# Sample tokens in four groups, their rows of u and v spread over all four stretches of a mixer

## Chip, core and metric

One core of a Trainium2 chip runs the whole program in one launch. The metric is the device time of that launch in microseconds (us).

## What is computed

One inference step of a two-layer encoder for 384 tokens: 256 of one prompt and 128 sample tokens (8 streams of 16). Layer 0 has a state-space block, layer 1 an attention block, and behind each stands the mixer that this change is about, with 16384 experts, each a row of a table `u` and a row of a table `v` of 1024 numbers:

```python
q = (xb @ w_q).reshape(PEER_TOKEN_BLOCK, PEER_HEADS, PEER_QDIM)
...
vs, ci = lax.top_k(cand, PEER_TOPK)
...
eid = (e1 * PEER_NKEYS + e2).reshape(PEER_TOKEN_BLOCK, PEER_HEADS * PEER_TOPK)
gate = jax.nn.softmax(vs.astype(jnp.float32), axis=-1).reshape(PEER_TOKEN_BLOCK, PEER_HEADS * PEER_TOPK)
ue = jnp.take(u_tab, eid, axis=0)
act = jax.nn.gelu(jnp.einsum('tkd,td->tk', ue, xb).astype(jnp.float32))
ve = jnp.take(v_tab, eid, axis=0)
return jnp.einsum('tk,tkd->td', (gate * act).astype(xb.dtype), ve)
```

Each token picks 128 experts, takes the product of each one's row of `u` with the token, and sums the rows of `v` with the weights that come out.

## The kernel before, in words

**The prompt's 256 tokens** go through all 16384 experts. The experts are a grid of 128 by 128; `e2` counts 128 slices of 128 experts, and `HE` is 64. A *u step* (`u_step`) multiplies one slice of `u` with the tokens and writes one of 64 rows of an expert grid, `G[0]` for the first 64 steps and `G[1]` for the other 64, each row 128 experts by 256 tokens. A *v step* (`v_step`) reads one row of the grid and adds its product with a slice of `v` to four accumulators in PSUM. So a mixer has 256 steps `s` in **four stretches** of 64: stretch 1 fills `G[0]`, stretch 2 `G[1]`, stretch 3 uses up `G[0]`, stretch 4 `G[1]`. Between the steps of stretch 2, every second step, `w_step` multiplies columns of `G[0]` with the gates of the experts that each token chose (0 elsewhere); in stretch 3 it does so for `G[1]`.

Numbers are kept at full precision by splitting: a slice of 512 KB is loaded to `raw` (three buffers, SP queue), ScalarE (ACT) rounds it to `hi` (L105), VectorE (DVE) makes the rest `lo` (L106), and TensorE (PE) multiplies three times: 24 products of 256 columns in a u step (L130 to L132), 12 of 512 columns in a v step (L143). Steps listed in `NATIVE` (8 of a mixer's first 64) multiply the raw slice without a split: 8 products (L1098), each of which the trace shows as 2.

**The 128 sample tokens** gather the rows that they chose. A *u item* is one gather of 128 rows (512 KB, issued by GpSimd, POOL, L1035) to one of three buffers `gath`, and one instruction of DVE that multiplies them with the tokens and sums (L1072). There are 128 of them in a mixer, in `GR` groups of tokens: a group's u items must all be done before `group_end` makes the coefficients of that group. A *quad* (`v_quad`) takes four gathers of rows of `v` and adds 8 products with small coefficient tiles to the banks `out_s` (L1089); there are 32 quads. Their buffers are `gv` (4) and later `gath`.

**Order.** Each engine runs its instructions in the order of its queue. Which step issues how many u items and quads is set in the code: `tick` issues `RATES` u items a step as soon as the routing of the sample tokens has ended (some 16 steps into stretch 1) until all 128 are done; `quads` issues one quad every 3.75 steps from the third step of stretch 3 to the end. The routing of the prompt's tokens (top 16 of scores and their decoding, all on DVE) is pulled in pieces between the steps of stretch 1. A scheduler with a model of the engines fixes the final order of what the code leaves open.

Of the kernel before, what the change touches and what calls it, by code (L numbers as in the profile page):

```python
# [9 lines left out]
F32 = mybir.dt.float32  # L10
# [9 lines left out]
P = 128  # L20
# [21 lines left out]
GR = 2  # L42
TG = P // GR
RG = 32 // GR
TURN = 6
GSCALE = 2.0 ** 15
NATIVE = range(4, 58, 7)
# [6 lines left out]
RATES = (0.95, 0.8, 0.8)  # L54
QUADS = (2, 3.75)
# [3 lines left out]
def encoder_step(ctx: ExitStack, tc: tile.TileContext, t_in, t_out):  # L59
# [750 lines left out]
    def peer(l):  # L810
        with ExitStack() as c:
# [32 lines left out]
            xg = [T(x0ctx.__enter__(), [P, D], F32, tag="xg0"), T(one, [P, D], F32, tag="xg1")]  # L844
# [13 lines left out]
            for g in range(GR):  # L858
                rows = xrow[g]
                pool.dma_start(xg[g], bass.AP(tensor=rows.tensor, offset=rows.offset, ap=[[0, GR], [D, TG], [1, D]]))  # L860

# [170 lines left out]
            pools = {}  # L1032
# [11 lines left out]
            def fetch_v(n):  # L1044

                if n < P:
                    r, q = divmod(n, 4)
                    if done["u"] == P and n % 7 >= 4:
                        tile_ = T(one, [P, D], F32, tag="gath", bufs=3)
                    else:  # L1050
                        tile_ = T(pools["gv"], [P, D], F32, tag="gv", bufs=4)
                    vrows[n] = gather(tile_, t_in["p_v"], eidT[:, 32 * q + r:32 * q + r + 1])
# [3 lines left out]
            def group_end(g, lay):  # L1056
# [5 lines left out]
                a = coef[g] = T(one, [P, TG], F32, tag="a", bufs=2)  # L1062
# [4 lines left out]
            def u_item(k):  # L1067
# [6 lines left out]
                if j == TG - 1:  # L1074
                    lay = T(one, [P, GR, TG], F32, tag="cm", bufs=2)
# [4 lines left out]
            def v_quad(r):  # L1080
# [5 lines left out]
                rows = [vrows.pop(4 * r + q) for q in range(4)]  # L1086
# [64 lines left out]
            due_u = [0.0]  # L1151

            def tick(rate):
                due_u[0] += rate
                while done["u"] < min(int(due_u[0]), P):
# [20 lines left out]
            for e2 in range(HE):  # L1176
# [170 lines left out]
```

## Time and profile before

| | us |
|---|---|
| Median of 3 runs (2600.17 to 2608.42) | 2606.8 |
| The profiled execution, whole | 2607.89 |
| Its span, first to last instruction | 2605.9 |
| Stretches 1, 2, 3, 4 of the first mixer | 224.4, 214.2, 251.5, 214.9 |
| The same of the second mixer | 228.6, 214.5, 256.2, 215.1 |

The profiled execution lies 1.1 us above the median; 2.0 us of it lie outside its span. The stretches are cut where the first steps of each begin on the engines, to within 3 us. What lies before, between and behind the mixers is the same code in both kernels.

### The profile page before, as it was taken

What the parts mean: (1) busy time and instruction counts of PE and PEld (TensorE: products, weight loads), DVE (VectorE), ACT (ScalarE), POOL (GpSimd) and SP (SyncE); (2) the same over time, 40 slices, a digit from 0 to 9 for tenths busy, and PEclk for the clock granted to TensorE, in tenths of its full rate; (3) what the DMA queues carried; (4) which work ended last, traced back from release to release, by engine and by line L of the source; (5) the groups of instructions that cost most, each with busy time, mean ns of one, the idle gap of its engine ahead of it and who ended that gap; (6) DMA issues with size and microseconds to landing.
All of it is one profiled execution on the core that took longest, in us unless ns stands there. A gap on an engine that the chain in (4) does not pass through costs nothing. (4 is left out here: it accounts for less than half of the span.)

```text
span 2605.9 us, 45142 instructions
## 1 busy us (share of the span) xinstructions
PE 2454.3 (94%) x16792; PEld 2076.6 (80%) x16792; DVE 1942.3 (75%) x4301; ACT 1324.6 (51%) x2562; POOL 671.6 (26%) x722
## 2 busy tenths in 40 slices
PE   7999999989899989999999899999889998899998
PEld 7999988988899966666667678998789986566666
DVE  6877737989899988765555555989989998665555
ACT  5665524433466655554444453434456766464444
POOL 2222200033322244333220000023332234432331
PEclk9999999999999999999999789999999999999999
DMA  5544434478788899888886204477788898988886
GB/s 181 175 150 174 147 133 146 157 274 282 262 302 292 293 338 344 333 306 301 328 299 182 77 30 148 135 260 279 258 281 282 295 337 314 340 295 301 320 322 235
DMA packets 180428, 645.62 MB, mean 248 GB/s; under 512 B 24496, under 2 KB 27664, under 8 KB 177552
## 3 DMA queue, kind: packets, MB, share of 16 engines
q1 hardware_dynamic: 102320, 372.16, 41.0%
q0 software_dynamic: 77888, 270.58, 29.8%
q8 instruction: 131, 2.15, 0.3%
q14 instruction: 89, 0.73, 0.1%
HBM read 626.43 MB, written 18.06 MB: 247 GB/s over the span
## 5 line engine op out<-in xcount | busy, mean ns | idle before, releaser
L105 ACT CAST hi<-raw 128x1024 fp32r<-128x1024 f32 (+1 forms) x616 | 641.4, 1042 | 657.7 <-PE bank L131 403.4
L106 DVE TENSOR_TENSOR lo<-raw,hi 128x1024 fp32r<-128x1024 f32 (+1 forms) x616 | 748.8, 1216 | 237.2 <-ACT hi L105 224.6
L1035 POOL DMA_INDIRECT gath<-in_p_u,eidU x256 | 303.7, 1186 | 804.2 <-DVE gath L1072 437.4
L132 PE MATMUL bank<-xhi,lo 128*128 128x256 f32 (+1 forms) x1344 | 408.6, 305 | 9.8 <-DVE lo L106 9.6
L130 PE MATMUL bank<-xhi,hi 128*128 128x256 f32 (+1 forms) x1344 | 404.4, 301 | 11.0 <-ACT hi L105 11.0
L131 PE MATMUL bank<-xlo,hi 128*128 128x256 f32 (+1 forms) x1344 | 398.9, 297 | 0.0
L132 PE MATMUL bank<-qhi,lo 128*128 128x256 f32 (+1 forms) x1152 | 350.2, 306 | 24.9 <-DVE lo L106 24.7
L130 PE MATMUL bank<-qhi,hi 128*128 128x256 f32 (+1 forms) x1152 | 349.7, 304 | 24.3 <-ACT hi L105 17.4
L1072 DVE SCALAR_TENSOR_TENSOR gath<-gath,xg 128x1024 f32<-128x1024 f32 x256 | 311.3, 1216 | 48.2 <-DMA gath<-in_p_u,eidU 48.1
L131 PE MATMUL bank<-qlo,hi 128*128 128x256 f32 (+1 forms) x1152 | 346.1, 300 | 0.0
L143 PE MATMUL bank<-lo,phi 128*128 128x512 f32 x1024 | 331.6, 405 | 10.6 <-DVE lo L106 7.7
L143 PE MATMUL bank<-hi,plo 128*128 128x512 f32 x1024 | 322.5, 397 | 0.0
L143 PE MATMUL bank<-hi,phi 128*128 128x512 f32 x1024 | 292.5, 406 | 16.0 <-ACT hi L105 12.2
L105 ACT CAST phi<-G 128x256 fp32r<-128x256 f32 x256 | 103.4, 405 | 376.1 <-PE bank L143 259.2
L1035 POOL DMA_INDIRECT gv<-in_p_v,eidT x180 | 196.1, 1089 | 321.9 <-PE bank L1089 271.5
L132 PEld LDWEIGHTS bank<-xhi,lo 128*128 128x128 f32 x1344 | 255.4, 190 | 18.2 <-DVE lo L106 15.0
L130 PEld LDWEIGHTS bank<-xhi,hi 128*128 128x128 f32 x1344 | 256.0, 190 | 16.3 <-ACT hi L105 13.1
L143 PEld LDWEIGHTS bank<-hi,phi 128*128 128x128 f32 x1024 | 186.7, 189 | 94.6 <-ACT hi L105 40.0
L131 PEld LDWEIGHTS bank<-xlo,hi 128*128 128x128 f32 x1344 | 255.9, 190 | 0.2
L132 PEld LDWEIGHTS bank<-qhi,lo 128*128 128x128 f32 x1152 | 224.8, 196 | 31.5 <-DVE lo L106 31.1
L130 PEld LDWEIGHTS bank<-qhi,hi 128*128 128x128 f32 x1152 | 225.4, 196 | 28.0 <-ACT hi L105 20.2
L143 PEld LDWEIGHTS bank<-lo,phi 128*128 128x128 f32 x1024 | 186.7, 189 | 70.0 <-DVE lo L106 17.4
(327 smaller groups left out, 3937.7 us busy)
## 6 DMA issues: line engine op xcount, KB each, us to landing
raw<-in_u_t SPq DMA_DIRECT2D x256, 512.0 KB
raw<-in_p_v SPq DMA_DIRECT2D x256, 512.0 KB
raw<-in_w_in SPq DMA_DIRECT2D x32, 512.0 KB
raw<-in_p_w_q SPq DMA_DIRECT2D x32, 512.0 KB
s<-in_state_ssm SPq DMA_DIRECT2D x8, 1024.0 KB
raw<-in_w_z SPq DMA_DIRECT2D x16, 512.0 KB
out_sm_ssm<-s SPq DMA_DIRECT2D x8, 1024.0 KB
raw<-in_w_out SPq DMA_DIRECT2D x16, 512.0 KB
```

Source lines behind the costliest of these rows:

```text
L105: act.copy(hi, raw)
L106: dve.tensor_tensor(lo, raw, hi32, op=OP.subtract)
L130: pe.matmul(ps, whi[:, s], xhi[:, k, c0:c1], start=(k == 0), stop=False)
L131: pe.matmul(ps, whi[:, s], xlo[:, k, c0:c1], start=False, stop=False)
L132: pe.matmul(ps, wlo[:, s], xhi[:, k, c0:c1], start=False, stop=(k == KD - 1))
L143: mm = pe.matmul(ps, x, w[:, hf * n:(hf + 1) * n], start=s_, stop=e_)
L1035: pool.indirect_dma_start(out=tile_, out_offset=None, in_=tab, in_offset=bass.IndirectOffsetOnAxis(ap=idx, axis=0))
L1072: pin(dve.scalar_tensor_tensor(tile_, tile_, 1.0, xg[g], op0=OP.mult, op1=OP.mult, accum_out=au[g][:, j:j + 1]))
```

## The change

Tokens of the samples stand in four groups of 32 in place of two of 64 (`GR`), and each group's token rows are loaded when the group two before it has ended (`load_group`), into the buffer that this one held. When a u item or a quad is issued is now a table by step: `U_DUE` asks for 26 u items by the end of stretch 1, 70 by the end of stretch 2, 106 by the end of stretch 3, and the rest by step 214; `V_DUE` places 5 quads at steps 82 to 106 (stretch 2), 8 at 148 to 186 (stretch 3) and 19 at 193 to 248 (stretch 4). Rows of `v` land in rows of the expert grid that hold nothing at that time: in stretch 2 in the last 16 rows of `G[1]`, which u steps fill from step 112 on, and from step 145 on in rows of `G[0]` that v steps have used up, 4 buffers first and 8 from step 164 on. The pool `gv` is gone, and so is the use of `gath` for `v`. `NATIVE` has 18 steps (every third) in place of 8. The banks `out_s` are taken at the start of stretch 2. The copies of the tokens that stretch 2 uses are spread over 8 steps, and the residual `h` comes back over POOL's queue in place of SP's.

```diff
-GR = 2
+GR = 4
-TURN = 6
+TURN = 8
-NATIVE = range(4, 58, 7)
+NATIVE = range(3, 56, 3)
-RATES = (0.95, 0.8, 0.8)
-QUADS = (2, 3.75)
+U_DUE = ((64, 26), (128, 70), (192, 106), (214, P))
+V_DUE = [82 + 6 * i for i in range(5)] + [148 + int(5.5 * i) for i in range(8)] + [193 + int(3.1 * i) for i in range(19)]
+V_FIRST = 5
...
-            xg = [T(x0ctx.__enter__(), [P, D], F32, tag="xg0"), T(one, [P, D], F32, tag="xg1")]
+            x0pool = x0ctx.__enter__()
...
+            def load_group(g):
+                xg[g] = T((x0pool, one)[g % 2], [P, D], F32, tag=f"xg{g % 2}", bufs=1)
                 rows = xrow[g]
                 pool.dma_start(xg[g], bass.AP(tensor=rows.tensor, offset=rows.offset, ap=[[0, GR], [D, TG], [1, D]]))
...
-            def fetch_v(n):
...
+            def fetch_v(n, s):
+
+                half, e = (1, HE - 16 + 4 * (n % 4)) if s < 2 * HE else (0, 4 * (n % v_bufs(s)))
+                assert all(k != (half, e) for k, _ in vrows.values())
+                tile_ = G[half][:, e:e + 4].rearrange("p e t -> p (e t)")
+                r, q = divmod(n, 4)
+                vrows[n] = (half, e), gather(tile_, t_in["p_v"], eidT[:, 32 * q + r:32 * q + r + 1])
+
+            def v_bufs(s):
+                return 4 if s < 2 * HE + 36 else 8
...
                 if j == TG - 1:
+                    if g + 2 < GR:
+                        load_group(g + 2)
...
-            def quads(e2):
-
-                while done["v"] < min(32, int((e2 - QUADS[0]) / QUADS[1] + 1)):
+            def quads(s):
+
+                while done["v"] < 32 and V_DUE[done["v"]] <= s:
                     v_quad(done["v"])
                     done["v"] += 1
-                    ahead = 4 * done["v"] + (7 if done["u"] == P else 4)
-                    while done["f"] < min(ahead, P):
-                        fetch_v(done["f"])
-                        done["f"] += 1
+                if s >= 2 * HE - 16 and done["f"] == 4 * V_FIRST and s < 2 * HE + 17:
+                    return
+                last = 4 * V_FIRST if s < 2 * HE else P
+                ahead = 4 * done["v"] + (4 if s < 2 * HE else v_bufs(s))
+                while done["f"] < min(ahead, last):
+                    fetch_v(done["f"], s)
+                    done["f"] += 1
...
-                    sync.dma_start(h, spill)
+                    pool.dma_start(h, spill)
```

Two places in the order of the engines. The first is DVE's queue in the middle of stretch 1 of the first mixer, where pieces of the prompt's routing stand between the splits of the slices (`lo<-raw,hi`) and the u items (`gath,au<-gath,xg`). Before:

```order
L874 MAX_INDEX CI_6252<-VS_6251,tk_1026_6310 128x8
L1072 SCALAR_TENSOR_TENSOR gath_6193,au_5499<-gath_6193,xg_635_4059 128x1024
L106 TENSOR_TENSOR lo_6505<-raw_6502,hi_6504 128x1024
L872 MATCH_REPLACE tk_1050_6451<-v_1049_6450,bank_6447 128x128
L870 MAX v_1049_6450<-bank_6447 128x8
L874 MAX_INDEX IX_6253<-v_1033_6354,tk_1040_6396 128x8
L1072 SCALAR_TENSOR_TENSOR gath_6316,au_5499<-gath_6316,xg_635_4059 128x1024
L894 TENSOR_TENSOR cand_6437<-v_1033_6354 128x32
L106 TENSOR_TENSOR lo_6575<-raw_6572,hi_6574 128x1024
```

Now:

```order
L1080 SCALAR_TENSOR_TENSOR gath_6183,au_5473<-gath_6183,xg_645_4125 128x1024
L902 TENSOR_TENSOR cand_6374<-v_1025_6294 128x32
L108 TENSOR_TENSOR lo_6413<-raw_6410,hi_6412 128x1024
L878 MAX VS_6141<-cand_6374 128x8
L108 TENSOR_TENSOR lo_6461<-raw_6458,hi_6460 128x1024
L879 MAX_INDEX CI_6142<-VS_6141,cand_6374 128x8
L880 MATCH_REPLACE tk_1038_6378<-VS_6141,cand_6374 128x88
L881 MAX VS_6141<-tk_1038_6378 128x8
L882 MAX_INDEX CI_6142<-VS_6141,tk_1038_6378 128x8
L878 MAX v_1042_6399<-bank_6396 128x8
L879 MAX_INDEX IX_6143<-v_1042_6399,bank_6396 128x8
```

Where two splits came with two u items, they come with one, and routing stands in the place of the other.

The second is POOL's queue in the first mixer, where each row is a gather of 512 KB (`x4`: four of them one behind the other), at the place where the gathers of `u` end. Before, that is in stretch 3:

```order
L1035 DMA gath_12113<-in_p_u,eidU_4006 128x1024
L1035 DMA gath_12138<-in_p_u,eidU_4006 128x1024
L1035 DMA gv_12083<-in_p_v,eidT_4011 128x1024
L1035 DMA gv_12085<-in_p_v,eidT_4011 128x1024
L1035 DMA gv_12087<-in_p_v,eidT_4011 128x1024
L1035 DMA gv_12089<-in_p_v,eidT_4011 128x1024
L1035 DMA gath_12379<-in_p_v,eidT_4011 128x1024
```

Now, in stretch 4, where the gathers of `u` go on to step 214:

```order
L1042 DMA G_619_4015<-in_p_v,eidT_4011 128x1024 x4
L1042 DMA gath_13307<-in_p_u,eidU_4006 128x1024
L1042 DMA gath_13346<-in_p_u,eidU_4006 128x1024
L1042 DMA gath_13371<-in_p_u,eidU_4006 128x1024
L1042 DMA G_619_4015<-in_p_v,eidT_4011 128x1024 x4
L1042 DMA gath_13396<-in_p_u,eidU_4006 128x1024
L1042 DMA gath_13435<-in_p_u,eidU_4006 128x1024
L1042 DMA gath_13460<-in_p_u,eidU_4006 128x1024
```

Before, only gathers of `v` follow from here to the end of stretch 4; now three gathers of `u` stand between each four of `v` in the first third of stretch 4, and the gathers of `v` write the grid.

## Rows read from the trace of the kernel before

**Rows 1.** Page: engine, busy time, share of the span and instructions.

```profile
PE 2454.3 (94%) x16792; PEld 2076.6 (80%) x16792; DVE 1942.3 (75%) x4301; ACT 1324.6 (51%) x2562; POOL 671.6 (26%) x722
```

**Rows 2.** Windows: mixer 1's stretches, mixer 2's first, third; length, busy, clock, DMA share, GB/s.

```profile
483.00:707.40 224.40, 204.49 (x1521) 196.49 (x1520) 202.72 (x650) 93.79 (x143) 68.35 (x49) 0.96 0.77 260
707.40:921.60 214.20, 207.59 (x2048) 202.09 (x2047) 198.95 (x306) 142.93 (x291) 56.57 (x56) 0.99 0.87 293
921.60:1173.10 251.50, 234.65 (x1517) 159.10 (x1518) 192.04 (x323) 143.27 (x282) 106.06 (x96) 0.99 0.90 331
1173.10:1388.00 214.90, 212.74 (x1026) 149.55 (x1025) 110.57 (x147) 94.25 (x133) 63.09 (x73) 1.00 0.85 302
...
1677.00:1905.60 228.60, 205.31 (x1519) 196.99 (x1519) 203.28 (x651) 93.41 (x143) 65.59 (x49) 0.96 0.75 256
...
2120.10:2376.30 256.20, 235.48 (x1517) 159.13 (x1518) 192.13 (x323) 143.09 (x281) 104.80 (x96) 0.98 0.89 325
```

**Rows 3.** Timeline of PE: start, length, instruction, at five places of mixer 1.

```profile
534.79 3.62 PE L1098 MATMUL bank<-xf,raw 128*128 128x256 f32 x16
...
538.37 0.28 PE L130 MATMUL bank<-qhi,hi 128*128 128x256 f32 x1
...
801.28 0.28 PE L130 MATMUL bank<-xhi,hi 128*128 128x256 f32 x1
...
803.65 0.28 PE L132 MATMUL bank<-xhi,lo 128*128 128x256 f32 x1
...
807.15 0.64 PE L1131 MATMUL bank<-og,oa 128*128 128x64 f16 x16
...
807.63 0.36 PE L132 MATMUL bank<-xhi,lo 128*128 128x256 f32 x1
...
1180.62 1.09 PE L143 MATMUL bank<-hi,phi 128*128 128x512 f32 x4
...
1183.42 1.09 PE L143 MATMUL bank<-hi,phi 128*128 128x512 f32 x4
...
1189.11 0.62 PE L1089 MATMUL bank<-gv,cm 128*32 128x512 f32 x2
...
1190.96 1.20 PE L143 MATMUL bank<-hi,phi 128*128 128x512 f32 x4
```

**Rows 4.** Windows, shorter: two parts of stretch 1, four of stretch 3.

```profile
483.00:532.60 49.60, 47.42 (x373) 46.00 (x372) 40.72 (x137) 23.63 (x34) 6.34 (x5) 1.00 0.64 217
532.60:707.40 174.80, 157.07 (x1151) 150.49 (x1150) 162.00 (x514) 70.16 (x110) 62.01 (x44) 0.95 0.80 272
...
920.00:940.00 20.00, 17.75 (x112) 12.62 (x111) 16.23 (x29) 11.24 (x23) 11.64 (x11) 1.00 0.99 372
...
977.20:1060.00 82.80, 76.29 (x479) 52.33 (x478) 69.64 (x117) 45.22 (x87) 42.96 (x36) 1.00 0.95 352
...
1040.00:1060.00 20.00, 19.02 (x89) 13.69 (x88) 15.12 (x23) 7.66 (x12) 12.59 (x10) 1.00 1.00 382
...
1100.00:1173.10 73.10, 73.10 (x460) 49.20 (x459) 47.92 (x77) 42.52 (x80) 21.38 (x22) 1.00 0.88 310
```

**Rows 5.** Groups by line on DVE: count, busy, mean ns; stretch 1 twice, stretch 3.

```profile
L106 DVE TENSOR_TENSOR lo<-raw,hi 128x1024 fp32r<-128x1024 f32 x56 | 68.0, 1215 | 1.9 <-ACT hi L105 1.8
L1072 DVE SCALAR_TENSOR_TENSOR gath<-gath,xg 128x1024 f32<-128x1024 f32 x46 | 55.7, 1212 | 15.6 <-DMA gath<-in_p_u,eidU 15.6
...
L1072 DVE SCALAR_TENSOR_TENSOR gath<-gath,xg 128x1024 f32<-128x1024 f32 x28 | 34.2, 1220 | 2.5 <-DMA gath<-in_p_u,eidU 2.5
```

**Rows 6.** Waits in stretch 1 of mixer 1: total us, times, longest.

```profile
ACT hi L105 <- DMA raw<-in_u_t: 24.4, 12, 3.7
...
PEld bank L132 <- DVE lo L106: 16.0, 15, 3.1
```

**Rows 7.** Windows of L1035, POOL's gathers: stretches 3 and 4, busy and count.

```profile
921.60:1173.10 251.50, 106.06 (x96) 0.99 0.90 331
1173.10:1388.00 214.90, 59.40 (x57) 1.00 0.85 302
```

More of the change, by code (lines that the diff above doesn't have):

```diff
@@ L1085, in v_quad @@
                                          op0=OP.is_equal, op1=OP.mult)
-                rows = [vrows.pop(4 * r + q) for q in range(4)]
+                rows = [vrows.pop(4 * r + q)[1] for q in range(4)]
                 for hf in range(2):
@@ L1150, in peer, with tick @@
             done = {"u": 0, "v": 0, "f": 0}
[L1151 to L1155, printed above, removed]
+            start = [0]
+            def tick(s):
+                s0, n0 = start[0], 0
+                for s1, n1 in U_DUE:
+                    if s < s1:
+                        break
+                    s0, n0 = s1, n1
+                want = P if s >= U_DUE[-1][0] else n0 + (n1 - n0) * (s + 1 - s0) // (s1 - s0)
+                while done["u"] < want:
                     fetch_u(done["u"] + 2)
@@ L1191, in peer @@
                     if not busy:
+                        start[0] = e2 + 1
                         fetch_u(0)
@@ L1202, in peer @@
             G[1] = T(gpools[1], [P, HE, NP], F32, tag="G1")
+            out_s = [bank([P, 512]) for _ in range(2)]
             for e2 in range(HE):
                 u_step(HE + e2)
-                tick(RATES[1])
+                tick(HE + e2)
                 if e2 % 2 == 1:
                     w_step(0, 8 * (e2 // 2))
-            assert done["u"] >= TG
+                if e2 >= 12:
+                    quads(HE + e2)
             xpool.__exit__(None, None, None)
-            x0ctx.__exit__(None, None, None)
             vpool = c.enter_context(tc.tile_pool(name="pv", bufs=1))
-            pools["gv"] = (gctx := tc.tile_pool(name="pgv", bufs=1, side="right")).__enter__()
-            out_s = [bank([P, 512]) for _ in range(2)]
-            for n in range(4):
-                fetch_v(n)
-            done["f"] = 4
+            h = None
             for e2 in range(2 * HE):
                 v_step(e2)
-                if e2 < HE:
-                    tick(RATES[2])
-                    if e2 % 2 == 1:
-                        w_step(1, 8 * (e2 // 2))
-                quads(e2)
-                if done["v"] == 32 and "gv" in pools:
-                    pools.pop("gv")
-                    gctx.__exit__(None, None, None)
+                if done["u"] < P:
+                    tick(2 * HE + e2)
+                elif h is None:
+                    x0ctx.__exit__(None, None, None)
                     h = open_h()
-                    sync.dma_start(h, spill)
+                    pool.dma_start(h, spill)
+                if e2 < HE and e2 % 2 == 1:
+                    w_step(1, 8 * (e2 // 2))
+                quads(2 * HE + e2)
             for b in DONE:
```

24 lines of the change are left out of this document (9 added, 15 removed).

## The prediction, as it was put on record

> **What bounds the kernel now.** I read the page's busy times first. PE is busy 2454.3 of 2605.9 us [rows 1], which looks like a kernel with no room; but its products overlap, so I took the distance from one start to the next from the timeline instead. In a row of products with nothing to wait for, 20 products of a u step take 803.65 - 801.28 = 2.37 us [rows 3], so its 24 take 2.84. A v step takes 1183.42 - 1180.62 = 2.80. The 16 products of a w_step take 807.63 - 807.15 = 0.48. A quad takes 1190.96 - 1189.11 = 1.85, with the change to it and back some 1.9. A NATIVE step starts at 534.79, and the second product behind it at 538.37; less one distance of 0.12 that is 3.46 us [rows 3]. From these I made a floor of PE for each stretch of a mixer and set it beside the stretch's length [rows 2]:
>
> - Stretch 1: 56 x 2.84 + 8 x 3.46 + some 6 for the routing's products = 193. It takes 224.4: 31 lost.
> - Stretch 2: 64 x 2.84 + 32 x 0.48 = 197. It takes 214.2: 17 lost.
> - Stretch 3: 64 x 2.80 + 32 x 0.48 + 16 quads x 1.9 = 225. It takes 251.5: 26 lost.
> - Stretch 4: 64 x 2.80 + 16 x 1.9 = 210. It takes 214.9: 5 lost.
>
> So the two mixers hold some 160 us that PE waits, and each stretch has another cause. In stretch 1 it is DVE: in its first 49.6 us, before u items begin, DVE is busy 40.7 (82%) and PE loses 3 us; in the 174.8 us behind, DVE is busy 162.0 (93%) [rows 4] and PE loses the other 28. PE's weight loads wait there for `lo`, and ACT also for `raw` [rows 6], whose buffers come free by the same DVE. In stretch 2 DVE has 199.0 us of work [rows 2] against PE's floor of 197: two equal engines, 17 lost. In stretch 3 it is the DMA: while u items and quads run together it moves 352 GB/s at a share of 0.95, in the fullest 20 us 372 and 382 at 0.99 and 1.00, and PE is idle there; when the u items are done, PE is busy without a gap at 310 GB/s [rows 4]. Stretch 4 is bound by PE.
>
> **The change, part by part**, for the first mixer. Counted from groups, 46 u items lie in stretch 1, 28 in stretch 3 [rows 5], and so 54 in stretch 2. The tables make that 26, 44, 36 and 22, and quads 5, 8 and 19 in place of 16 and 16.
>
> *Stretch 1.* DVE loses 20 u items and, by 10 more NATIVE steps, 10 splits, each 1.21 us [rows 5]: 36 us. PE gains 10 x (3.46 - 2.84) = 6, and 1 for more small products with four groups. In the part with u items (48 steps, 13 of them NATIVE, were 6) PE's floor is 35 x 2.84 + 13 x 3.46 + 6 = 150; DVE has 162.0 - 20 x 1.21 - 7 x 1.21 = 129, or 86%. With 82% PE lost 6% of its floor, with 93% it lost 20% [rows 4]; I take 8%, near the first: 162. The first part becomes 11 x 2.84 + 5 x 3.46 + 3 lost = 52. Together 214: **-10**. Bounds: 200 if nothing waits, and 231 (+7) if the 31 us stay although DVE has less to do. A slice for a NATIVE step holds its `raw` buffer until PE has used it, and the SP queue, in order, holds the next load behind it; two splits a period of three steps (9.1 us of PE) leave time for that, so I cost it within the 8%.
>
> *Stretch 2.* It gains 5 quads, 5 x 1.9 = 9.5, and 1 us of group ends: floor 208. DVE falls to 199.0 - 10 x 1.21 + 1 = 188, 90% of it. Between that 82% and the 101% of today I take 10 us lost: 218, **+4**. Bounds: 208 (-6) and 225 (+11, the 17 as now). Behind a quad that waits for its gather on PE stand the next step's products; the gathers have six steps (20 us) for four rows, so this wait should be short. The Gelu of step 112 waits for the last quad at step 106, six steps before. The two banks that `out_s` takes earlier cost nothing: six are left, and stretches 3 and 4 run with two.
>
> *Stretch 3.* Eight quads less: floor 225 - 8 x 1.9 = 210. DVE has 192.0 + 8 x 1.21 - 2 = 200, DMA 76 gathers in place of 96 [rows 7]: 251.5 us x 331 GB/s = 83.2 MB less 20 x 0.524 = 72.7 MB. At 352 GB/s that is 207 us. All three engines come near 210; I take the 17 us that stretch 2 loses now with two equal engines: 227, **-25**. Bounds: 216 (-35; loss as in stretch 4) and 241 (-10; 31 lost, as in stretch 1).
>
> *Stretch 4* pays. It gets 22 u items less 2 fetched ahead, and 68 gathers of `v`: 88 where it has 57 [rows 7]. 214.9 x 302 = 64.9 MB become 64.9 + 31 x 0.524 = 81.1 MB. PE's floor is 64 x 2.80 + 19 x 1.9 = 215.3. In steps 192 to 213 a step asks for one slice, one row of `u` and 4 / 3.1 of `v`, 1.72 MB in some 3.4 us, over 500 GB/s, which no row shows; eight buffers carry two quads of it. POOL's gathers of `u` stand behind those of `v` there, which wait for quads; DVE waits for the u row, its split stands behind, and PE behind that. So the DMA ends last: at 352 GB/s, the row where both kinds run as here, 81.1 MB take 231 us: **+16**. Bounds: 219 (+4, PE's floor and a small loss; the DMA would have to hold 370) and 268 (+54, at 302 GB/s). DVE, 110.6 + 22 x 1.21 = 137 us, has room.
>
> *At nothing:* the reload of a group's token rows is issued when its buffer falls free, a whole group of 32 items before it is read; behind it on POOL stand gathers that wait for the same item anyhow. The load of `h` is now last on POOL, behind gathers that end two quads (20 us) before the end; without that cover it would be 1.5 MB at 352 GB/s, 4 us a mixer. The ACT copies are as many as before.
>
> The sum: -10 + 4 - 25 + 16 = -15 us. The second mixer's stretches 1 and 3 take 4 and 5 us longer than the first's now [rows 2], in the very waits that shrink; I take half of that more, -20. 2607.9 - 35 = **2573 us** for the profiled execution; the median of before is 1.1 us lower, which I leave.
>
> One rule speaks against it. The fullest rows show 372 and 382 GB/s with a share of 0.99 and 1.00 [rows 4]. The Trainium skill, DMA: Bandwidth & Descriptors, Specifications, gives some 358 GB/s as what the memory gives one core. By that rule, at the share of 0.90 that stretch 3 has on average, stretch 4 would get an estimated 322 GB/s, and 81.1 MB would take 252 us, +37, so that the sum would be +6 and +1, near nothing. The trace is above that limit for 20 us at a time, so I don't go by it; its mechanism is the first rival.
>
> **The rivals.**
>
> *The DMA can't carry stretch 4 (slower).* If two kinds of gathers and the slices together get no more than the 302 GB/s that stretch 4 moves today, it takes 268 us, +54: -10 + 4 - 25 + 54 = +23 and +18, 2607.9 + 41 = 2649. It decides from where stretch 4 eats the other three, 215 + 31 = 246 us, or 330 GB/s. For it: stretches 3 average 331 and 325 [rows 2], and a starved PE falls idle in steps that nothing gives back. Against it: 352 over 83 us, and the 302 is no limit, since PE hardly waits in that stretch.
>
> *Stretch 1 keeps its waits (no change).* If the late slices [rows 6], not DVE, hold it, the NATIVE steps cost their 7 us and give nothing: +7 + 4 - 25 + 16 = +2, then -3: 2607. For it: 24.4 us of ACT's waits there name the load of `raw`. Against it: DVE at 93%, and the same loads with DVE at 82% lose 3 us.
>
> *Everything runs as its free parts do (faster still).* Stretch 1 loses 6% in all (-15), stretch 2 is at 213 (-1), stretch 3 at 219 (-32), and stretch 4 holds 370 GB/s (+4): -44 and -48: 2516. For it: PE without a gap in the last 73 us of stretch 3 at 310 GB/s [rows 4]. Against it: three engines near their limit in stretch 3.
>
> **How the numbers follow.** The forecast's case has 0.57, the slower rival 0.12, the no-change rival 0.12, the faster one 0.19. The forecast's own range is 2540 to 2600 (stretch bounds half used, alike in both mixers). Over all the cases 2522 to 2610 leaves out half of the faster rival and the slower one, 2 in 10. A measurement of this kernel can tell 0.3%, 8 us. Faster: 0.56 of the forecast's case and the faster rival, and 0.02 of the no-change one, 0.77. Same: 0.10. Slower: 0.13.
>
> **What would show it.** Stretch 1 near 214 us with DVE's busy share under 85% and fewer waits for `lo`; stretch 3 near 227; stretch 4 near 231 with a DMA share over 0.9 and 350 GB/s, and PE's gaps in its first third, released by gathers of `v` and of `u`. The step that could be most wrong is stretch 4: over 246 us the change loses. If stretch 1 stays at 224 or more, DVE was not what held it.

## The result, and the profile after

The changed kernel is 0.6% slower: median 2619.3 us of 7 runs (2610.1 to 2634.3) beside 2608.0 us of 7 runs of the kernel before, ratio 1.0059 with a 95% interval of 1.0033 to 1.0085. The forecast was 2573, 0.77 for faster.

The profiled execution took 2616.46 us, its span 2614.8. PE, which had 2454.3 us of busy time [rows 1], has 13 more, DVE 18 less. (PE's busy time also grows where its clock falls: with the same products, the run without reloads below has 2448.3.)

```profile
PE 2467.6 (94%) x16728; PEld 2087.6 (80%) x16728; DVE 1924.8 (74%) x4293; ACT 1304.7 (50%) x2546; POOL 683.4 (26%) x728
```

The stretches tell more. These windows of the changed kernel have the columns of [rows 2]: stretches 1 to 4 of mixer 1, then 1 and 2 of mixer 2.

```profile
492.60:697.00 204.40, 200.19 (x1454) 191.36 (x1453) 171.43 (x590) 80.33 (x131) 35.59 (x29) 0.99 0.68 235
697.00:938.30 241.30, 224.60 (x2134) 210.73 (x2132) 188.84 (x291) 144.15 (x293) 66.24 (x66) 0.96 0.85 283
938.30:1163.40 225.10, 215.25 (x1393) 157.71 (x1394) 195.83 (x330) 143.89 (x281) 94.90 (x75) 0.98 0.88 321
1163.40:1397.50 234.10, 221.42 (x1082) 150.11 (x1081) 136.50 (x199) 93.36 (x133) 100.90 (x105) 1.00 0.93 349
1688.40:1895.60 207.20, 201.87 (x1454) 192.03 (x1453) 171.86 (x590) 79.91 (x131) 37.64 (x29) 0.98 0.67 231
1895.60:2133.90 238.30, 223.25 (x2134) 209.55 (x2132) 188.72 (x291) 144.11 (x293) 68.00 (x66) 0.97 0.86 287
```

From here on a stretch is cut alike in all kernels, at the end of ACT's write of the first, 64th and 128th row of the grid and of its 64th and 128th cast of a row. By that cut stretch 1 of the kernel before is 221.7, 2.7 less than its window in [rows 2], which begins earlier. Mixer 1 and mixer 2:

| us | stretch 1 | stretch 2 | stretch 3 | stretch 4 | all four |
|---|---|---|---|---|---|
| before | 221.7 / 226.0 | 214.2 / 214.5 | 251.5 / 256.3 | 214.9 / 215.1 | 902 / 912 |
| after | 204.4 / 207.2 | 241.2 / 238.2 | 225.1 / 228.8 | 234.1 / 237.0 | 905 / 911 |
| difference | -17 / -19 | **+27 / +24** | -26 / -27 | +19 / +22 | +3 / -1 |
| forecast, first mixer | -10 | +4 | -25 | +16 | -15 |

Stretches 1 and 3 went as forecast or better, and stretch 4 took 3 and 6 us more than put. Stretch 2 took the whole gain back. The other 7 us of this profile lie ahead of mixer 1, which begins at 492.6 and not at 485.7. Among the kernels below, whose code ahead of it is the same, it begins between 486.1 and 497.0, so I take most of that as scatter.

Two readings of the trace gave me the suspects. The first is the reload of a group's token rows (L865), one of which starts at 725.55. The first fence is the timeline of POOL, ACT, DVE and PE around it (start, length, instruction; in brackets the idle time ahead of it and what ended that). The second is the window of the 14 us behind it.

```profile
725.55 0.73 POOL L865 DMA_DIRECT2D xg<-xrow  x1 [3.79 <-DVE gath L1080]
...
739.64 1.04 ACT L107 CAST hi<-raw 128x1024 fp32r<-128x1024 f32 x1 [7.68 <-DMA raw<-in_u_t]
...
740.72 1.22 DVE L108 TENSOR_TENSOR lo<-raw,hi 128x1024 fp32r<-128x1024 f32 x1 [5.68 <-ACT hi L107]
...
740.74 0.58 PE L132 MATMUL bank<-xhi,hi 128*128 128x256 f32 x1 [2.86 <-ACT hi L107]
```

```profile
726.00:740.00 14.00, 11.88 (x124) 11.67 (x122) 7.53 (x12) 4.81 (x10) 3.13 (x4) 1.00 0.93 237
```

A slice comes late, ACT waits 7.7 us for it, DVE for ACT, PE for both, and the DMA engines are busy 93% of the time for only 237 GB/s, where stretch 3 before moved 352 at 95% [rows 4]. Later in the stretch there is a second reload, at 906.28.

The second is a quad with its gathers, at 766. DVE's multiplication of the grid, L1143, waits for the 16 products of a w_step on PE (L1141) and for nothing else. The timeline of PE, POOL, ACT and DVE there:

```profile
766.38 1.92 PE L1099 MATMUL bank<-G,cm 128*32 128x512 f32 x16
...
771.58 0.35 PE L1141 MATMUL bank<-og,oa 128*128 128x64 f16 x6
...
768.55 0.94 POOL L1042 DMA_INDIRECT G<-in_p_v,eidT  x1 [3.82 <-PE bank L1099]
...
773.61 0.93 POOL L1042 DMA_INDIRECT gath<-in_p_u,eidU  x1 [0.30 <-issue]
...
774.35 1.05 ACT L107 CAST hi<-raw 128x1024 fp32r<-128x1024 f32 x1 [3.33 <-remote]
...
775.45 0.39 PE L132 MATMUL bank<-xhi,hi 128*128 128x256 f32 x1 [0.60 <-issue]
...
775.81 0.69 DVE L1143 SCALAR_TENSOR_TENSOR G<-bank,G 128x512 f32<-128x512 f32 x1 [5.79 <-PE bank L134]
...
777.15 0.81 PE L1141 MATMUL bank<-og,oa 128*128 128x64 f16 x16 [1.19 <-DVE og L1124]
```

The products end at 771.93 by the records, yet L1143 begins at 775.81, 3.88 us later. From 768.55 to 774.54 POOL issues four gathers of `v` and one of `u`. ACT is late as well: the cast at 774.35, whose releaser the profile does not name, needs a buffer `hi` that PE read last at 771.62 by the records, and its slice had landed at 768.9. PE's gap of 0.60 us ends with that cast. Behind L1143 on DVE stands `og`, and PE waits 1.19 us for that. Then the clock falls. Windows of 774.6 to 777.7 and of what follows, the granted clock third from the end:

```profile
774.60:777.70 3.10, 1.30 (x20) 0.92 (x19) 1.89 (x4) 2.47 (x5) 0.00 (x0) 1.00 1.03 402
777.70:784.50 6.80, 6.13 (x34) 5.97 (x31) 5.02 (x8) 2.84 (x7) 0.94 (x1) 0.50 0.86 295
784.50:795.00 10.50, 10.50 (x101) 8.93 (x99) 8.88 (x13) 6.12 (x13) 1.87 (x2) 1.00 0.78 247
```

PE was busy 1.30 of 3.10 us, and for the next 6.8 us it ran at 0.50, the lower level of 1.2 GHz; u products stand 0.21 us apart there instead of 0.12. The same follows the reload's gap:

```profile
740.70:747.00 6.30, 5.80 (x25) 5.50 (x26) 4.73 (x7) 3.58 (x10) 0.87 (x1) 0.50 0.61 209
```

### The profile page after: what moved, and what is told of

Read it like the earlier page. It is cut to its first block, busy times and chain, and to the rows that moved or that the text cites. A ratio compares the mean times of both kernels' runs of the same rounds, so it can differ in the third digit from the quotient of the medians.

```text
span 2614.8 us, 44999 instructions
## 1 busy us (share of the span) xinstructions
PE 2467.6 (94%) x16728; PEld 2087.6 (80%) x16728; DVE 1924.8 (74%) x4293; ACT 1304.7 (50%) x2546; POOL 683.4 (26%) x728
## 3 DMA queue, kind: packets, MB, share of 16 engines
q0 software_dynamic: 78240, 275.82, 29.8%
## 4 chain that ended last, share of the span: by engine, by line
PE 72%; DVE 11%; DMA 9%; issue 3%; ACT 3%; POOL 1%; another core or an unknown queue 1%; SPq 0%; ACTq 0%; POOLq 0%; DVEq 0%
PE bank L145 26%; PE bank L134 9%; PE bank L132 9%; PE bank L133 9%; DVE lo L108 4%; PE bank L1099 4%; PE bank L1108 3%; DMA raw<-in_u_t 3%; DMA gath<-in_p_u,eidU 2%; ACT hi L107 2%; PE bank L1141 2%; DVE gath L1080 1%; PE bank L525 1%; PE bank L428 1%; PE bank L429 1%
## 5 line engine op out<-in xcount | busy, mean ns | idle before, releaser
L107 ACT CAST hi<-raw 128x1024 fp32r<-128x1024 f32 (+1 forms) x596 | 619.6, 1042 | 668.9 <-PE bank L133 283.0
L108 DVE TENSOR_TENSOR lo<-raw,hi 128x1024 fp32r<-128x1024 f32 (+1 forms) x596 | 724.3, 1216 | 259.0 <-ACT hi L107 253.2
L132 PE MATMUL bank<-xhi,hi 128*128 128x256 f32 (+1 forms) x1344 | 411.0, 306 | 15.6 <-ACT hi L107 14.7
L1042 POOL DMA_INDIRECT G<-in_p_v,eidT x256 | 287.6, 1123 | 304.0 <-PE bank L1099 212.2
L132 PE MATMUL bank<-qhi,hi 128*128 128x256 f32 (+1 forms) x992 | 303.1, 306 | 13.2 <-ACT xf L854 7.6
L134 PE MATMUL bank<-qhi,lo 128*128 128x256 f32 (+1 forms) x992 | 297.2, 301 | 4.8 <-DVE lo L108 4.7
L133 PE MATMUL bank<-qlo,hi 128*128 128x256 f32 (+1 forms) x992 | 296.1, 299 | 0.0
L145 PEld LDWEIGHTS bank<-hi,plo 128*128 128x128 f32 x1024 | 193.9, 189 | 43.3
L108 DVE TENSOR_TENSOR plo<-G,phi 128x256 fp32r<-128x256 f32 x256 | 108.1, 423 | 146.8 <-PE bank L145 130.6
```

The source lines that it names most:

```text
L107: act.copy(hi, raw)
L108: dve.tensor_tensor(lo, raw, hi32, op=OP.subtract)
L132: pe.matmul(ps, whi[:, s], xhi[:, k, c0:c1], start=(k == 0), stop=False)
L133: pe.matmul(ps, whi[:, s], xlo[:, k, c0:c1], start=False, stop=False)
L134: pe.matmul(ps, wlo[:, s], xhi[:, k, c0:c1], start=False, stop=(k == KD - 1))
L145: mm = pe.matmul(ps, x, w[:, hf * n:(hf + 1) * n], start=s_, stop=e_)
```

## Experiments: what holds stretch 2

**No reload.** Groups 2 and 3 use the rows of groups 0 and 1.

```diff
-                        load_group(g + 2)
+                        xg[g + 2] = xg[g]
```

> The changed kernel without the two later loads of token rows in each mixer (groups 2 and 3 are multiplied with the rows of groups 0 and 1). Theory R, the reload of token rows slows every transfer beside it and PE waits for slices: stretch 2 falls from 241 and 238 us to some 230, the whole by about 20 us to 2600. Theory B, the four gathers of a quad in a row starve the slices: stretch 2 stays at 238 or more, the whole within 4 us of 2619. Theory Q, a quad's products and gaps alone: as B.

Measured: stretch 2 230.0 and 232.1 us, -11 and -6; the whole 0.9969 (0.9938 to 1.0) of the kernel before. The reload's cost is real, and not all.

**Rows of quad 0 used five times.** 16 of the 20 gathers in stretch 2 are left out; the quads stay.

```diff
+                if 4 <= n < 4 * V_FIRST:
+                    vrows[n] = (half, e), tile_
+                    return
```

> The changed kernel with 4 gathers of v in stretch 2 in place of 20: quads 1 to 4 multiply the rows of quad 0. Theory B (gathers of four starve the slices): stretch 2 falls by 10 to 14 us a mixer, to 228, the whole to some 2595. Theory R (reload): stretch 2 falls by 3 us at most. Theory Q (the quads' products on PE, which stay here): no change.

Measured: 228.6 and 229.2, -13 and -9; the whole 0.9959 (0.9932 to 0.9987). The quads' gathers cost as much as the reloads.

**Gathers one by one.** If four in a row on POOL's queue are the trouble, spreading them should help.

```diff
-                while done["f"] < min(ahead, last):
-                    fetch_v(done["f"], s)
-                    done["f"] += 1
+                for _ in range(1 if s < 2 * HE else 2):
+                    if done["f"] < min(ahead, last):
+                        fetch_v(done["f"], s)
+                        done["f"] += 1
```

> The changed kernel with all its gathers, but those of v put one (stretch 2) or two (stretches 3 and 4) at a step into POOL's queue, in between those of u, in place of four in a row. Theory B: stretch 2 falls by 6 to 10 us a mixer and stretch 4 by some 5, the whole to 2590 to 2600. Theory R and theory Q: no change beyond 4 us; if the bytes alone count in stretch 4, it stays at 234.

(All gathers are also pinned to their places in POOL's queue.) Measured: 242.5 and 240.6, nothing gained; 1.0066 (1.004 to 1.0093). It isn't the row of four: L1143 starts late here too, by 9.7 and 9.3 us in all in pieces of 1.0 to 2.6, where the changed kernel has 11.7 and 8.7 in pieces of 1.5 to 3.9. (Counted are starts more than 1 us behind the last product, without those at the stretch's first w_step, beside the gathers of quad 0, which none of these cuts takes out.) The granted clock in that stretch is 0.99 here, so the clock is not the whole of it either: PE waits 11.8 us for `lo` instead, where it waited 6.9.

**Both cuts at once.**

> The changed kernel with both cuts at once: the two reloads of token rows in a mixer left out (groups 2 and 3 use the rows of groups 0 and 1), and quads 1 to 4 use the rows of v that quad 0 gathered (16 of the 20 gathers in stretch 2 left out). Alone the first gave stretch 2 = 230.0 and 232.1 us in the two mixers, the second 228.6 and 229.2, against 241.2 and 238.2 with neither. Theory A (two separate losses): both go, stretch 2 is 217 to 220 and 222 to 224, close to the 218 of the prediction, and the whole is near 2580. Theory S (one shared loss, of which either cut takes away the same part, such as the memory's bandwidth): stretch 2 stays at 226 to 229 and the whole near 2597.

Measured: 219.2 and 219.4, the whole 2577.0, 0.986 (0.9837 to 0.9883). The two losses add up (-22 and -19, where the two cuts alone sum to -24 and -15), and without them stretch 2 is what the prediction said, 218. PE's clock is at 1.00 throughout:

```profile
695.50:914.70 219.20, 215.23 (x2134) 203.48 (x2132) 188.82 (x291) 144.23 (x293) 48.79 (x48) 1.00 0.81 270
```

**As many bytes without an index.** Without reloads, and the rows of quads 1 to 4 come by plain loads on the same queue.

```diff
+                if 4 <= n < 4 * V_FIRST:
+                    pool.dma_start(tile_, t_in["p_v"][l * NKEY * NKEY + 777 * n:l * NKEY * NKEY + 777 * n + P, :])
+                    vrows[n] = (half, e), tile_
+                    return
```

> Without the reloads, and the 16 gathers of quads 1 to 4 in stretch 2 are plain loads of 128 consecutive rows of v, in the same place of the same queue, into the same buffers: as many bytes, no row by row addresses from an index. The rows are not the chosen ones. Beside the kernel without reloads (stretch 2 of 230.0 and 232.1). Theory B (the bytes or the wait for them cost): stretch 2 stays at 229 to 233. Theory G (GpSimd's work for an indexed gather disturbs the other engines): stretch 2 falls to 218 to 223, and the grid's multiplications on DVE (L1143) follow the products they wait for without the 2 to 4 us of lag.

Measured: 219.5 and 220.2, as without these transfers. The bytes cost nothing, though the stretch moves 307 GB/s. And L1143 (L1147 in this kernel) starts right behind its products. Windows of the stretch, then PE and DVE around one quad:

```profile
693.90:913.50 219.60, 215.53 (x2134) 203.61 (x2133) 188.75 (x291) 144.07 (x293) 57.97 (x64) 1.00 0.88 307
```

```profile
759.27 2.20 POOL L1058 DMA_DIRECT2D G<-in_p_v  x4 [3.85 <-PE bank L1103]
...
762.27 0.35 PE L1145 MATMUL bank<-og,oa 128*128 128x64 f16 x6
...
762.66 0.69 DVE L1147 SCALAR_TENSOR_TENSOR G<-bank,G 128x512 f32<-128x512 f32 x1 [1.95 <-PE bank L1145]
```

The products end at 762.62, and DVE begins at 762.66: 0.04 us, not 3.88. The same count over the whole stretch gives no late start here, none with the rows of quad 0 used five times and none in the kernel before; the run without reloads, with all its gathers, has 8.4 and 9.9 us of them.

**As many indexed gathers, a sixteenth of the bytes.**

```diff
+                if 4 <= n < 4 * V_FIRST:
+                    pool.indirect_dma_start(out=tile_[:, :64], out_offset=None, in_=t_in["p_v"].rearrange("r (c f) -> (r c) f", f=64),
+                                            in_offset=bass.IndirectOffsetOnAxis(ap=eidT[:, 32 * q + r:32 * q + r + 1], axis=0))
```

> Without the reloads, and the 16 gathers of quads 1 to 4 in stretch 2 fetch 64 numbers of a row in place of 1024: as many indexed gathers in the same place of the queue, a sixteenth of the bytes. The sums of v are not the right ones. Beside the kernel without reloads (230.0 and 232.1). Theory B (the bytes cost): stretch 2 falls to 218 to 223. Theory G (the indexed gather's work on GpSimd costs): it stays at 228 to 233.

Measured: 223.9 and 225.3, between the two theories: 4.7 and 5.9 us above no gathers, where whole rows cost 10.8 and 12.7. So some half of the gathers' price comes with the index itself; the other half only when whole scattered rows move. Neither comes with the bytes alone. L1143's late starts shrink alike, to 3.2 and 4.5 us. (The plain loads read 128 rows in a row, so an index and scattered rows are not told apart.)

**Four copies of the token rows.** With 8 `NATIVE` steps, and each reload reads 128 different rows.

```diff
+                if g >= 2:
+                    pool.dma_start(xg[g], xrep[g - 2].rearrange("i c r d -> (i c r) d"))
+                    return
...
+            xrep = T(dram, [2, GR, 4, RG, D], F32, tag=f"xrep{l}")
+            for c4 in range(4):
+                for i in range(GR):
+                    pool.dma_start(xrep[:, i, c4], xn[2][32 * c4 + 16:32 * c4 + 32])
```

> The changed kernel with 8 NATIVE steps, and the token rows of groups 2 and 3 are written to memory four times at the start of the mixer, so that each reload reads 128 different rows where it read the same 32 rows four times; nothing is left out. With 8 NATIVE steps alone: stretch 1 199.7 and 200.0, stretch 2 238.5 and 240.4, stretch 4 237.6 and 235.7. Theory R1 (a reload is slow, and slows the slices beside it, because it reads the same rows four times): stretch 2 falls by 7 to 11 to 229 to 232, and the whole is 0.6% to 0.9% below the kernel before. Theory R2 (any such transfer at that place costs as much, by its bytes or its place in the queue): stretch 2 stays at 238 to 241, and the whole is within 0.3% of the kernel before.

Measured: the whole is 2590.4, 0.9904 (0.9883 to 0.9926), faster than both kernels and with nothing left out. At the reload itself it came as theory R1 has it. The step in which the late slice shows took 8.4 us (9.3 in mixer 2) with 8 `NATIVE` steps alone, and takes 3.2 (3.3) with four copies; in the 14 us behind the reload PE has no gap and the DMA moves 320 GB/s at 91%:

```profile
720.00:734.00 14.00, 14.00 (x132) 13.95 (x131) 12.16 (x20) 9.50 (x21) 2.81 (x3) 1.00 0.91 320
```

The edit changed the form of the load as well as its rows, though. By the pages of the changed kernel and of the one without reloads (78240 and 76128 packets of this queue) each of the four reloads is 528 packets, some 400 of them under 512 bytes, where 128 rows of 4 KB make 128; with four copies most of the small ones are gone (513 packets of 4 bytes from 722 to 740 us there, 164 from 716 to 734 here). Whether the repeated rows or the small packets hold up the slices isn't separated.

In the profiled executions the stretch fell by only 2.0 and 6.0, to 236.5 and 234.4. The two don't compare well: this one took 2604.85 us, 14 above its median, and that with 8 `NATIVE` steps alone 2595.34, 16 below its own. By the ratios of the whole, 0.9999 and 0.9904, four copies give 25 us for both mixers, above R1's 7 to 11 a mixer. And the quads cost more in this execution: L1143's late starts are 14.0 and 12.6 us, against 9.8 and 12.0. It shows the same chain as above, twice over:

```profile
689.10:925.60 236.50, 223.16 (x2134) 209.78 (x2132) 188.67 (x291) 144.47 (x292) 65.16 (x66) 0.97 0.85 289
...
785.00:788.80 3.80, 1.77 (x18) 1.66 (x17) 1.41 (x3) 2.04 (x4) 0.94 (x1) 1.00 0.91 344
788.80:795.60 6.80, 6.28 (x41) 6.12 (x41) 5.50 (x9) 2.55 (x7) 0.94 (x1) 0.50 0.82 291
```

At a mean clock of 0.97 that is some (1 - 0.97) x 236.5 = 7 us of clock, where the kernels without these gathers and reloads are at 1.00.

**A later multiplication of the grid.** As the kernel with four copies, but the multiplication follows the next w_step's `og`, and was meant to hold neither that nor the split behind it. (Unlike what its expectation says, one thing changes: the first row that stretch 4 reads lacks the gates of the last eight tokens.)

```diff
+                with tc.issue_after(og.ins):
+                    w_end()
...
-                dve.scalar_tensor_tensor(gv, ps.rearrange("p t e -> p e t"), 1.0 / GSCALE, gv, op0=OP.mult, op1=OP.mult)
+                late.append((gv, ps))
```

> As the kernel with four copies, and the multiplication of the grid at the end of each w_step (L1143 of the changed kernel) stands behind the next w_step's first two instructions on DVE, 6 us later, so that a late signal of its products holds neither these two nor the splits behind them. Nothing is left out. Theory H (the gathers of v cost stretch 2 their 11 us by holding this one instruction back, and through it DVE's queue): stretch 2 is 5 to 11 us shorter than with four copies alone, 220 to 226 if that is 229 to 232. Theory I (the gathers hold back PE's signals to every engine, not this one instruction): stretch 2 is within 3 us of it.

Measured: 238.1 and 238.1 against 236.5 and 234.4; the whole 0.9935 (0.9912 to 0.9958). But this does not settle theory H, since the edit doesn't free DVE's queue. `og` has one buffer, which PE reads in the same 16 products (L1150 here), so the next `og` waits for them as the multiplication did:

```profile
784.83 0.49 PE L1150 MATMUL bank<-og,oa 128*128 128x64 f16 x11
...
789.19 0.69 DVE L1131 TENSOR_TENSOR og<-ob,g 128x1024 f16<-128x1024 f16 x1 [5.75 <-PE bank L134]
```

The last product ends at 785.32, `og` begins at 789.19, 3.87 us later: the wait has moved to another instruction at the same place.

**No w_steps in stretch 2.** From the kernel with four copies.

> The kernel with four copies (stretch 2 of 236.5 and 234.4), with the w_steps of stretch 2 left out: the first half of the grid isn't multiplied by the gates, so the prompt's result is not the right one; u steps, u items, quads and their gathers stay. PE's floor of stretch 2 becomes 64 x 2.84 + 9.3 for the quads + 1.6 for the groups' ends = 193. Theory W (the indexed gathers cost stretch 2 only where they stand beside w_steps, whose links from PE to DVE and back have no slack): 195 to 200. Theory E (the gathers hold PE's signals back for every step): the steps at the quads stay 3 us or more above their work, and the stretch takes 205 or more.

Measured: 209.5 and 210.6, in theory E's range; DVE is at 62%, and still 17 us lie over PE's floor of 193:

```profile
687.50:896.90 209.40, 197.99 (x1622) 187.44 (x1620) 130.51 (x164) 85.95 (x132) 73.51 (x66) 0.99 0.91 327
...
779.60 0.38 ACT L1118 ACTIVATE G<-bank 128x256 f32<-128x256 f32 x1 [2.46 <-PE bank L134]
779.88 1.04 ACT L107 CAST hi<-raw 128x1024 fp32r<-128x1024 f32 x1
...
780.97 0.39 PE L132 MATMUL bank<-xhi,hi 128*128 128x256 f32 x1 [1.41 <-ACT hi L107]
```

It shows less than theory E says. Three times in each mixer PE stands 1.4 us, and 0.76 behind it, since the cast of the next slice stands on ACT behind the write of the grid that waits for PE's step: some 6.5 us of the 17 come from the order of a queue in this kernel. And no run without w_steps is also without gathers, so what the rest would be isn't known.

## Experiments: the other stretches

**18 `NATIVE` steps alone, in the kernel before; 8 of them in the changed one.**

```diff
-NATIVE = range(4, 58, 7)
+NATIVE = range(3, 56, 3)
```

> The kernel before with 18 NATIVE steps in place of 8, nothing else. Theory D (DVE bounds stretch 1): DVE loses 12 us, PE gains 6; stretch 1 falls from 222 and 226 us by 5 to 9, the other stretches stay, the whole by 10 to 18 us to 2590 to 2598. Theory L (late slices bound stretch 1, the raw buffers that NATIVE steps hold): stretch 1 rises by up to 6 us, the whole by up to 12.

```diff
-NATIVE = range(3, 56, 3)
+NATIVE = range(4, 56, 7)
```

> The changed kernel with NATIVE at 8 steps of stretch 1, as before, in place of 18; nothing is left out. Theory U (fewer u items alone free DVE in stretch 1): stretch 1 stays near 204 to 209 us, since 10 more splits of 1.21 us are 12 us of DVE, which has room, and PE saves 6. Theory N (the NATIVE steps are needed to get DVE under PE): it is 214 or more. The other stretches as in the changed kernel (241, 225, 234); the whole 2615 to 2625 by U, 2640 by N.

Measured: alone they give stretch 1 of 225.1 and 224.0, no gain (the whole 1.0024, 0.9997 to 1.0051). Taken back from the changed kernel, stretch 1 is 199.7 and 200.0, **shorter** by 5 and 7. (The whole is 2611.4, 0.9999 with 0.9968 to 1.003, in ten runs that scatter from 2595 to 2630.) Stretch 1 of the first mixer in the two:

```profile
488.40:713.50 225.10, 205.71 (x1432) 194.08 (x1431) 192.77 (x630) 81.53 (x130) 62.55 (x50) 0.97 0.76 262
...
488.20:687.90 199.70, 193.81 (x1534) 187.87 (x1534) 180.41 (x600) 90.74 (x140) 41.62 (x29) 1.00 0.70 240
```

Fewer u items freed stretch 1, and the ten steps cost their 10 x 0.62 us of PE and gave nothing back.

**Other rates of u items in the kernel before.**

```diff
-RATES = (0.95, 0.8, 0.8)
+RATES = (0.55, 0.84, 0.85)
```

> The kernel before with other rates of u items alone, 0.55, 0.84 and 0.85 a step in place of 0.95, 0.8 and 0.8: 26 items in stretch 1 where 46 were, 54 in stretch 2 as before, 48 in stretch 3 where 28 were; two groups, 8 NATIVE steps and quads as before; nothing is left out. Theory U (stretch 1 gains by having fewer u items and by nothing else): stretch 1 is 200 to 207 (221.7 and 226.0 before), stretch 2 within 3 us of 214, and stretch 3, which gets 20 gathers or 10.5 MB more where the DMA is the limit, takes 266 to 280 for 251.5 and 256.3; the whole is within 0.5% of the kernel before. Rival (the four groups' order of the routing is needed for the gain): stretch 1 at 214 or more.

Measured: stretch 1 209.2 and 205.9, stretch 3 276.6 and 281.5, both within 2 us of the ranges expected; the whole the same, 1.0 (0.9976 to 1.0023). Stretch 2, expected within 3 us of 214, is 206.9 and 207.5, 7 us less with as many items of its own. In the kernel before, the difference lies at the start of that stretch, where PE is busy 18.40 of 22.60 us:

```profile
707.40:730.00 22.60, 18.40 (x171) 17.43 (x171) 19.93 (x32) 11.52 (x25) 10.79 (x9) 0.92 0.81 288
```

So it had paid for something that stretch 1 left over; what, isn't shown.

**No gathers of `u` in stretch 4.**

```diff
-                if k < P:
+                if k < 106:
...
+                if k >= 106:
+                    src = xg[g]
```

> The changed kernel without the gathers of u for items 106 to 127, those of stretch 4: these items multiply the token rows with themselves, so that DVE does the same work; the sums of these items are not the right ones. Stretch 4 now takes 234.1 and 237.0. Theory D (the transfers of stretch 4 end last, as the prediction put it): 20 gathers of 0.524 MB less, 10.5 MB or 30 us at 352 GB/s, and stretch 4 falls to PE's floor and a small loss, 217 to 221. Theory Q (the 19 quads and the multiplications on DVE cost it, not the bytes): it stays at 229 or more.

Measured: 216.3 and 217.2, -18 and -20, with PE busy without a gap, although the 68 gathers of `v` stay:

```profile
1160.80:1377.10 216.30, 216.30 (x1082) 151.49 (x1081) 135.80 (x199) 94.73 (x134) 79.41 (x84) 1.00 0.89 324
```

**No quads in stretch 2, two groups.** If a quad in stretch 2 is dear, the change should spread u items only, and needs neither four groups nor reloads.

```diff
-GR = 4
+GR = 2
...
-NATIVE = range(3, 56, 3)
+NATIVE = range(4, 56, 7)
...
-U_DUE = ((64, 26), (128, 70), (192, 106), (214, P))
-V_DUE = [82 + 6 * i for i in range(5)] + [148 + int(5.5 * i) for i in range(8)] + [193 + int(3.1 * i) for i in range(19)]
-V_FIRST = 5
+U_DUE = ((64, 26), (128, 82), (192, 112), (205, P))
+V_DUE = [148, 152, 156, 160, 164] + [167 + 3 * i for i in range(8)] + [193, 197, 201] + [208 + int(2.6 * i) for i in range(16)]
+V_FIRST = 0
```

> The changed kernel with two groups in place of four (so no reloads), 8 NATIVE steps, no quads in stretch 2, and other tables: 26 u items by the end of stretch 1, 82 by the end of stretch 2, 112 by the end of stretch 3, the rest by step 205; 13 quads in stretch 3 and 19 in stretch 4. Nothing is left out. Theory K (the quads of stretch 2, at (235 - 207) / 5 = 5.6 us each, are what the change should not have made; u items alone can be spread): stretch 1 199 to 206, stretch 2 206 to 212, stretch 3, by 1.3 us a u item and 4.4 a quad from the runs so far, 225 + 5 x 4.4 - 6 x 1.3 = 239, stretch 4 227 to 233; some 876 a mixer where the kernel before takes 902 to 912: 2555 to 2570, 1.6% to 2.1% below it. Rival (the quads taken out of stretch 2 cost as much in stretch 3, where the DMA is full): stretch 3 at 250 or more, and the whole 0.5% to 1% below, as with four copies.

> As the one with no quads in stretch 2, with 32, 88 and 116 u items by the ends of stretches 1, 2 and 3, the rest by step 203, and 11 quads in stretch 3, 21 in stretch 4. Nothing is left out. By the prices so far (a u item 1.0 us in stretch 1, 0.9 in stretch 4, 1.3 in stretch 3; a quad 4.4 in stretch 3, 1 to 2 in stretch 4): stretch 1 +6, stretch 3 -9 to -12, stretch 4 -4 + 3, so 3 to 6 a mixer below the other. If stretch 4 with more quads in fewer steps is bound by the DMA again, it takes 240 or more and the two are the same.

Measured: the first 2577.1, 0.9905 (0.9877 to 0.9932), with stretches of 199.6, 207.0, 244.9, 246.2 in mixer 1 and 199.5, 207.2, 238.9, 242.7 in mixer 2. So stretch 2 came as priced for theory K, stretch 3 within 6 us of its 239, and stretch 4, with its 16 items in 13 steps, 10 to 19 us longer than put. By that the whole is 0.95% below the kernel before, where the rival had it, and not the 1.6% to 2.1% of theory K; but the rival's sign, stretch 3 at 250 or more, isn't there. The second, with more items early and fewer quads in stretch 3, is the best kernel here, **2567.9, 0.9853 (0.9828 to 0.9877)**:

```profile
488.00:701.90 213.90, 199.12 (x1511) 192.74 (x1510) 185.56 (x609) 90.47 (x140) 47.66 (x35) 0.97 0.69 239
701.90:909.20 207.30, 204.24 (x2040) 199.89 (x2038) 199.38 (x308) 142.83 (x292) 57.84 (x57) 1.00 0.90 305
909.20:1138.70 229.50, 222.91 (x1433) 157.16 (x1434) 188.54 (x315) 143.37 (x280) 96.32 (x77) 0.99 0.88 321
1138.70:1377.80 239.10, 231.12 (x1110) 151.01 (x1109) 126.00 (x180) 92.99 (x133) 97.62 (x104) 1.00 0.91 338
```

Its stretch 1 shows how steep the price of u items is there: six more than in the first one cost 14 us, not 6. Its mixers take 890 and 891 us (898 and 888 in the first one); 32 items in stretch 1 were too many, and something between 26 and 32 would be tried next.

## Why the prediction was wrong

**Stretch 2 is the step that failed: +4 forecast, +27 and +24 measured.** Counted from the 207 us of the kernels without quads there and without stretch 1's left-over work:

| | us, mixer 1 / 2 | put at |
|---|---|---|
| five quads' own products and groups' ends, 219.2 - 207 | 12 / 12 | 10.5, right |
| indexed gathers of `v`, 230.0 - 219.2 | 10.8 / 12.7 | nothing: "this wait should be short" |
| reloads, 241.2 - 230.0 | 11.2 / 6.1 | nothing: "a whole group of 32 items before it is read" |
| the 17 us lost before | 7 fell away | "10 us lost" of 17, right in size |

Each row is a difference of single executions. Stretch 2 with the same code took 242.0 and 245.4 in the run without late gathers of `u`, so a row can be some us off. The ratios of the whole agree in order: from 1.0059 to 0.9969 without reloads (23 us for both mixers), 0.9959 with rows once (26) and 0.986 with both (52).

I asked of the reload only whether its reader would wait for it. Its reader never did. The slices beside it did, since the DMA engines were busy beside it at 237 GB/s. And of the gathers I asked only whether the quad on PE would wait for its rows. It did not; instead the steps behind a quad ran late. The bound of 225 was built from the losses of a stretch without quads and could not contain either. The 10 us lost are right by luck: I took them from DVE's relief, from 199 to 188 us, yet the kernels without quads in stretch 2 lose the same 10 with DVE at 199 us (the window of 701.90 above). The 7 that fell away lay in the first 23 us of the stretch.

**Stretch 1: -10 forecast, -17 and -19.** The direction was right, and PE's waits for `lo` fell from the 16.0 us of [rows 6] to 2.4 in mixer 1. The loss was mis-sized: PE lost 207.1 - 199 = 8 us by the cut of [rows 2] (floor 46 x 2.84 + 18 x 3.46 + 6), where I allowed 15. And DVE's busy share, by which I sized it, does not rank the losses. With 8 `NATIVE` steps in the changed kernel DVE is busy 90% of the stretch (180.41 of 199.70), as much as before (202.72 of 224.40), and PE loses 9 us by the same cut, not 31; with 18 in the kernel before it is busy 86%, and PE loses 29. That fewer u items free the stretch is shown; whether by DVE's time, by their gathers or by their place in its queue, no run tells apart. The NATIVE steps cost the 6 us that I had put, but their ten splits did not have to go. The rival "stretch 1 keeps its waits" falls: ACT still waits 43.3 us for `raw` there, more than the 24.4 of [rows 6], and the stretch is shorter all the same.

**Stretch 3: -25 forecast, -26 and -27.** 225.1 at 321 GB/s, with PE busy 215 us, DVE 196 and the DMA for a share of 0.88. The size is right; which of the three holds the stretch, no run here tests.

**Stretch 4: +16 forecast, +19 and +22.** The runs bear out that the DMA ends last: without the 22 late gathers of `u` the stretch falls to 216.3, PE's floor, with the gathers of `v` still there. PE waited for `hi` and `lo` (5.9 and 5.3 us in mixer 1), most of it in the first third. The stretch moved 349 GB/s, against the 352 that I took. Its first third and the rest:

```profile
1163.40:1240.00 76.60, 67.12 (x321) 43.58 (x323) 53.38 (x83) 26.82 (x38) 49.30 (x40) 1.00 1.01 395
1240.00:1397.50 157.50, 154.29 (x765) 106.53 (x758) 83.12 (x116) 66.54 (x95) 51.61 (x66) 1.00 0.89 326
```

The first rival, at 302 GB/s, falls, and so does the rule beside it. The Trainium skill (DMA: Bandwidth & Descriptors, Specifications) gives some 358 GB/s as the memory's limit for a core, and this trace moves 395 for 76.6 us; the measurement decides.

**The sum.** Stretch 2 alone came 23 and 20 us longer than put, for both mixers 43 together. That is the distance from 2573 to the 2616.5 of the profiled execution. The rest nearly cancels: stretch 1 gave 7 and 9 more, stretch 4 took 3 and 6 more, 7 came ahead of mixer 1, and the 5 more that I had given the second mixer are not in this count by stretch. (In the faster rival 6% of a floor of 199 us makes -13 for stretch 1, not the -15 put; nothing hangs on it.) None of my rivals had stretch 2 as its place: all three argued over the engines that were already full, and none over the transfers that the change added.

**Open:** by what way an indexed gather delays PE's readers. DVE begins the multiplication of the grid 3.88 us after the last product that it waits for, as the records stand, and not so with plain loads. ACT's cast at 774.35 is late as well, by 2.73 us, so more than one link is. Whether DVE's queue or ACT's carries the most of the cost isn't shown: the run that was to free DVE's queue moved the wait with it, and the one without w_steps has gaps of its own. Whether PE's signal or PE itself is late the records can't tell, since the ends of its products are modelled.

## What to carry to other kernels

A transfer that nobody waits for can still have a price: ask which loads share the DMA engines and the queue with it in those microseconds, and what bytes per second it lets them have. Price work that moves into a stretch by running that stretch's work without its transfers, and with plain ones, before placing it there; the bound built here from rows of a stretch that had none of it did not hold. Before a run that moves an instruction is taken as a test, see whether the one in its place waits for the same thing. Where one stretch leaves work over for the next, relief in the first shows up in the second: fewer u items in stretch 1 of the kernel before gave 7 us in stretch 2 too, and spreading them, without the quads in stretch 2, was the part of this change that was worth keeping.

## What the runs showed of the hardware that I had not expected

- Beside a load that reads the same 32 rows of 4 KB four times the DMA engines were busy without moving much: 237 GB/s at a share of 0.93 over 14 us, with slices beside it. With 128 different rows, as many bytes, it was 320 GB/s at 0.91. The first form also has some 400 small packets.
- Sixteen indexed gathers of 128 rows of 4 KB cost stretch 2 10.8 and 12.7 us, the same bytes by plain loads 0.3 and 0.8, and indexed gathers of 256-byte rows 4.7 and 5.9.
- Two short gaps of PE (0.60 and 1.19 us, within 3.10 us in which it was busy 1.30) were followed by 6.8 us at a granted clock of 0.50. So a gap here can cost more than its length. Not every one does: in the run with both cuts PE waits 1.5 us once, and the clock of the stretch stays at 1.00.
